# An encoder block on one core: both made-up weight sums are prepared in earlier stages and read back, and four more pairs of the down projection go by seven products

## The chip, the core and the metric

The kernel runs on one NeuronCore of a Trainium2 chip. The metric is the device time of one execution in microseconds (us). Five engines work side by side, each on its own list of instructions in order, and wait for each other by semaphores: TensorE (PE, with its weight loads as PEld), VectorE (DVE), ScalarE (ACT), GpSimd (POOL) and SyncE (SP). In this kernel SP and POOL issue the DMA transfers that matter here.

## The reference

One layer of an encoder on 256 tokens of width 2048, all in float32:

```python
h = rms_norm(x, attn_norm[i])
proj = h @ w_in[i]                                   # 10240 columns
ya = windowed_gqa(qa, ka, va, table, sink)
yb = dilated_attention(qb, kb, vb, table)
merged = sigmoid(ga) * (ya @ w_branch_a) + sigmoid(gb) * (yb @ w_branch_b)
x = x + merged @ w_out
hf = rms_norm(x, ffn_norm)
g = dwconv_centred(hf @ w_ffn_gate, conv_w, conv_b)  # 5632 columns
x = x + (gelu(g) * (hf @ w_ffn_up)) @ w_ffn_down     # down: 5632 -> 2048
gate_p = sigmoid(rms_norm(x, ple_norm) @ w_ple_gate)
x = x + gate_p * (p @ w_ple_proj)
return rms_norm(x, final_norm)
```

## The kernel before

Every float32 product is made of two halves of each operand: a rounded high half (`hi`) and the rest (`lo`). So each weight that is streamed from memory is split once: ACT copies it to `hi` (tiles `uh`, `vh`, line 305), DVE subtracts to get `lo` (tiles `ul`, `vl`, line 306), and PE multiplies with both. `thirds` is one product of a 128 x 128 block of the left side with 128 x 512 of the weights: three matmuls, lines 408 to 410 (`sh` by `wh`, `sh` by `wl`, `sl` by `wh`).

The weights come in 258 pieces of 128 x 2048 (1 MB), in the order in which they are used. SP loads a piece into one of three buffers `raw`; a piece's buffer is free for the piece three later when the last split of it is done. A piece is cut into units, and a unit's halves lie in a ring: six places for plain units (`u`), two for units that are made of sums (`v`). `pump` writes the splits into the program as soon as the ring has a place, and a scheduler then sets the final order on each engine, so a split can stand a long way ahead of its product.

The stages follow each other: A (projection and attention), B0 to B3 with ba and bb (gates and branches), D0 and D1 (output projection), E0 (first half of gate and up), F00 and F01 (first half of the down projection, to the left and the right 1024 columns), E1, F10 and F11 (second half), pp0 and pp1, G0, G2, G3 (the last gate). A down stage F works through 11 pieces, each a pair of k blocks by two blocks of 512 columns. A piece of kind `s` takes eight products (24 matmuls). A piece of kind `Z` takes seven (21 matmuls) by the method of Strassen and Winograd: M1 to M7, into seven PSUM banks, from four quarters of the weights and three sums of them, and from sums of the activations (`S`, made by `sums_of`). `DOWN` says which pieces are which.

For a Z piece one sum of three quarters is made ahead, in an earlier stage that has room: `sum_ahead` loads half of three quarters (POOL, line 268), two DVE additions make the sum (lines 271 and 272), POOL stores it in memory (line 275). One such half is an "ask" here. SP later reads the sum back into the first quarter of `raw` (line 255), beside the 768 KB of the other quarters (line 254). `sums_of_weights` makes the other three: line 282 makes the second quarter's (512 columns, after the quarter itself has been split as the piece's first unit), line 283 the third's and fourth's (1024 columns). The units of a Z piece are then: quarter 1 (512 columns), quarters 2 and 3 as they are (1024), `T21` (the first two sums) and `T03` (the last two). Asks run in stage A (16 of them, for D0 and D1), E0 (24, for F00 and F01) and E1 (28, for F10, F11 and G0), at most one for each job, a job being one block of 128 columns, 16 k blocks long. The buffers of the asks alternate between two places.

Of the kernel before, what the change touches and what calls it, by code (L numbers as in the profile page):

```python
# [16 lines left out]
P = 128  # L17
T = 256
# [77 lines left out]
DOWN = ("ZZsZsZsZsZs", "ZsZsZsZsZss")  # L96
# [97 lines left out]
def _encoder(ctx: ExitStack, tc, xt, pt, xrow, cols, gainrow, table, onehot, mask, ident_in, wts, out):  # L194
# [67 lines left out]
    def sum_ahead(p, h, tag):  # L262

        cols = slice(h * T, (h + 1) * T)
        if h == 0:
            ahead[p] = dram.tile([P, WIDE], F32, name="ahead%d" % p)
# [3 lines left out]
        def add():  # L270
            keep(nc.vector.tensor_tensor(q[:, 0], q[:, 2], q[:, 0], op=ALU.subtract))  # L271
            keep(nc.vector.tensor_tensor(q[:, 0], q[:, 0], q[:, 1], op=ALU.add))

        def store():
            keep(nc.gpsimd.dma_start(ahead[p][:, cols], q[:, 0]))
# [3 lines left out]
    def sums_of_weights(raw):  # L279

        q = [raw[:, i * WIDE:(i + 1) * WIDE] for i in range(4)]
        nc.vector.tensor_tensor(q[1], q[0], q[1], op=ALU.subtract)  # L282
        nc.vector.tensor_tensor(raw[:, 2 * WIDE:], raw[:, 2 * WIDE:], view(q[0], 0, (0, 2), (1, WIDE)), op=ALU.subtract)

    def produce():
# [13 lines left out]
        if kind == "T21" and not behind:  # L299
# [6 lines left out]
        nc.vector.tensor_tensor(lo, src, hi.bitcast(F32), op=ALU.subtract)  # L306
        if behind and u == _UNITS_OF[p][1]:
# [107 lines left out]
    def quad_stage(stage, moving, combos=None, tags=("M2", "M3", "M4", "P22")):  # L415
# [24 lines left out]
        for i, p in enumerate(pieces):  # L440
# [12 lines left out]
            else:  # L453
                s = combos(i)
                sums = [(s[:, 0, e], s[:, 1, e]) for e in range(4)]
# [37 lines left out]
    def gather(acc, scale=1.0, u=None, keep=lambda ins: ins):  # L493
# [3 lines left out]
        if u is None:  # L497
            u = sc.tile([P, T], F32, name="u")
# [32 lines left out]
    def diagonal(r):  # L531

        dg = sc.tile([P, T], F32, name="rdg", bufs=1)
# [316 lines left out]
    todo = [(p, h) for s in range(2) for p in _STAGES["D%d" % s] if _PIECES[p][0] == "Z" for h in range(2)]  # L850
# [67 lines left out]
    def sums_of(u, tag, s=None):  # L918
# [8 lines left out]
        if s is None:  # L927
            s = tok.tile([P, 2, 4, P], FR, name="S", tag="S%d" % tag)
        nc.scalar.activation(s[:, 0], f, AF.Copy)
        nc.vector.tensor_tensor(s[:, 1], f, s[:, 0].bitcast(F32), op=ALU.subtract)  # L930
# [120 lines left out]
    def places(half):  # L1051
# [6 lines left out]
        for i in seven[2:]:  # L1058
            d = act[:, at_:at_ + 14 * P].rearrange("p (c b t) -> p c b t", c=2, t=P)
            found[i] = lambda d=d: (d[:, :, :3], d[:, :, 3:])  # L1060
            at_ += 14 * P
        for i in eight[:-4]:
# [4 lines left out]
        for j, i in enumerate(seven[:2]):  # L1067
            found[i] = lambda j=j: (tok.tile([P, 2, 3, P], FR, name="ends", tag="S%d" % (2 + j)),
                                    tok.tile([P, 2, 4, P], FR, name="S", tag="S%d" % j))
        for j, i in enumerate(eight[-4:]):  # L1070
# [60 lines left out]
    ph_, pl_ = [], []  # L1131

# [4 lines left out]
    def split_last():  # L1137
        for k in range(2):
            ph_.append(sc.tile([P, T], FR, name="t"))
            pl_.append(sc.tile([P, T], FR, name="u"))  # L1140
            nc.scalar.activation(ph_[k], held["pr"][:, k], AF.Copy)
            nc.vector.tensor_tensor(pl_[k], held["pr"][:, k], ph_[k].bitcast(F32), op=ALU.subtract)
# [5 lines left out]
    for half in range(2):  # L1148
# [19 lines left out]
        if half:  # L1168
            at(("F10", 2, 0), load_last)
            at(("F10", 9, 0), split_last)  # L1170
# [26 lines left out]
    class Rows:  # L1197
# [3 lines left out]
        def __getitem__(self, i):  # L1201
            c = i[1]
            h = (ph_, pl_)[c.start >= T][self.k]
# [112 lines left out]
```

## Time and profile before

| | |
|---|---|
| runs | 1454.99 us median of 3 (1454.16 to 1456.2) |
| the profiled execution | 1455.38 us, its span 1453.6 us |
| granted TensorE clock | 0.998 |
| PE busy | 1442.5 us, 7470 matmuls |
| DVE busy | 1225.8 us |
| ACT busy | 827.7 us |
| POOL busy | 95.0 us |
| bytes moved | 318.57 MB, 219 GB/s on average |

The span is the time from the first to the last instruction; what the execution has beyond it (1.8 us) lies around the program. A row of the groups reads: line, engine, operation, tile written <- tiles read, shape, count | busy us, mean ns of one | idle time of the engine just before, and what ended it. Matmuls overlap in the records (each is shown with some 390 ns and the next begins before that), so the rate of PE is read from starts, not from durations. Waits of a matmul can also stand at its weight load (PEld).

### The profile page before, as it was taken

How to read it: one execution, taken by the hardware profiler on the slowest of the kernel's cores; microseconds unless marked ns; L12 is line 12 of the kernel's file. 1: busy time of each engine (PE TensorE's matmuls, PEld its weight loads, DVE VectorE, ACT ScalarE, POOL GpSimd, SP SyncE). 2: the span in 40 equal slices, each digit the busy share in tenths (PEclk: the TensorE clock that was granted, in tenths of full speed). 3: DMA queues.
4: the chain of work that ended last, by engine and by line, in shares of the span. 5: the costliest groups of instructions: out<-in, count | busy, mean ns of one | idle time of the engine just before them, and what ended most of it. 6: DMA issues, size and time to landing. Idle time of an engine off the chain costs nothing.

```text
span 1453.6 us, 19872 instructions
## 1 busy us (share of the span) xinstructions
PE 1442.5 (99%) x7470; PEld 1234.2 (85%) x7470; DVE 1225.8 (84%) x1754; ACT 827.7 (57%) x1148; POOL 95.0 (7%) x145
## 2 busy tenths in 40 slices
PE   9999999999999999999999999999999999999997
PEld 8888888888888888888888888888888888888885
DVE  7678775679998989889877999997878799998994
ACT  7455544546555655656545566465645466555753
POOL 0001120000000000000221100000221200000000
PEclk9999999999999999999999999999999999999999
DMA  9765575435556456465777655466776765556461
GB/s 331 273 211 201 199 262 188 172 142 203 188 190 233 179 217 238 174 253 209 270 238 273 237 210 194 189 249 226 265 281 236 261 241 213 199 196 233 173 249 69
DMA packets 62236, 318.57 MB, mean 219 GB/s; under 512 B 7668, under 2 KB 12660, under 8 KB 34236
## 3 DMA queue, kind: packets, MB, share of 16 engines
q1 hardware_dynamic: 50540, 280.46, 53.5%
q0 software_dynamic: 10880, 35.66, 6.8%
q8 instruction: 58, 0.95, 0.3%
q10 hardware_dynamic: 720, 1.19, 0.2%
q14 instruction: 38, 0.31, 0.1%
HBM read 306.23 MB, written 11.05 MB: 218 GB/s over the span
## 4 chain that ended last, share of the span: by engine, by line
PE 98%; DMA 0%; issue 0%; SPq 0%; ACT 0%; DVE 0%; POOLq 0%; POOL 0%; DVEq 0%
PE bank L351 29%; PE bank L358 15%; PE bank L408 14%; PE bank L409 14%; PE bank L410 14%; PE bank L397 2%; PE bank L399 2%; PE bank L398 2%; PE bank L335 2%; PE bank L336 1%; PE bank L947 1%; PE bank L756 0%; DMA raw<-in_wts 0%; PE bank L704 0%; PE bank L703 0%; PE bank L702 0%
## 5 line engine op out<-in xcount | busy, mean ns | idle before, releaser
L305 ACT ACTIVATE uh<-raw 128x1024 fp32r<-128x1024 f32 (+2 forms) x519 | 517.9, 1010 | 307.3 <-PE bank L410 112.5
L306 DVE TENSOR_TENSOR ul<-raw,uh 128x1024 fp32r<-128x1024 f32 (+2 forms) x519 | 594.6, 1164 | 95.7 <-ACT uh L305 66.8
L351 PE MATMUL bank<-hf,uh 128*128 128x512 f32 x1408 | 336.6, 391 | 0.0
L351 PEld LDWEIGHTS bank<-hf,uh 128*128 128x128 f32 x1408 | 258.8, 188 | 50.5 <-ACT uh L305 0.3
L358 PEld LDWEIGHTS bank<-hf,ul 128*128 128x128 f32 x1408 | 180.4, 191 | 6.7
L358 PE MATMUL bank<-hf,ul 128*128 128x256 f32 x1408 | 182.8, 283 | 0.0
L305 ACT ACTIVATE vh<-raw 128x1024 fp32r<-128x1024 f32 x96 | 100.9, 1056 | 55.5 <-DVE raw L282 27.8
L306 DVE TENSOR_TENSOR vl<-raw,vh 128x1024 fp32r<-128x1024 f32 x96 | 116.3, 1219 | 0.9
L351 PE MATMUL bank<-hs,uh 128*128 128x512 f32 x432 | 103.6, 392 | 0.0
L351 PEld LDWEIGHTS bank<-hs,uh 128*128 128x128 f32 x432 | 79.5, 188 | 15.6
L410 PE MATMUL bank<-uh,act 128*128 128x512 f32 x218 | 84.9, 390 | 0.0
L409 PE MATMUL bank<-ul,act 128*128 128x512 f32 x218 | 84.8, 389 | 0.0
L408 PE MATMUL bank<-uh,act 128*128 128x512 f32 x218 | 84.6, 390 | 0.0
L496 ACT ACTIVATE t<-bank 128x256 f32<-128x256 f32 x122 | 45.4, 374 | 59.1 <-PE bank L358 50.0
L408 PE MATMUL bank<-uh,hs 128*128 128x512 f32 x172 | 67.3, 392 | 0.0
L410 PE MATMUL bank<-uh,hs 128*128 128x512 f32 x172 | 67.2, 390 | 0.0
L409 PE MATMUL bank<-ul,hs 128*128 128x512 f32 x172 | 67.0, 389 | 0.0
L1092 ACT ACTIVATE gw<-gw,cl 128x256 f32<-128x256 f32 x44 | 24.1, 594 | 70.9 <-DVE gw L1089 70.8
L268 POOL DMA_DIRECT2D ahead<-in_wts x52 | 38.8, 747 | 379.0 <-DMA ahead<-ahead 210.0
L271 DVE TENSOR_TENSOR ahead<-ahead 128x256 f32<-128x256 f32 x52 | 22.0, 422 | 47.5 <-DMA ahead<-in_wts 47.4
L358 PE MATMUL bank<-hs,ul 128*128 128x256 f32 x432 | 56.6, 284 | 0.0
L358 PEld LDWEIGHTS bank<-hs,ul 128*128 128x128 f32 x432 | 54.5, 191 | 1.0
(270 smaller groups left out, 2454.1 us busy)
## 6 DMA issues: line engine op xcount, KB each, us to landing
raw<-in_wts SPq DMA_DIRECT2D x217, 1024.0 KB, 5.0
raw<-in_wts SPq DMA_DIRECT2D x34, 768.0 KB, 5.3
ahead<-in_wts POOLq DMA_DIRECT2D x52, 384.0 KB, 5.5
raw<-ahead SPq DMA_DIRECT2D x34, 256.0 KB, 5.3
ahead<-ahead POOLq DMA_DIRECT2D x52, 128.0 KB, 4.4
raw<-in_wts SPq DMA_DIRECT2D x12, 512.0 KB, 6.8
hb<-in_wts POOLq DMA_DIRECT2D x16, 384.0 KB, 5.4
ahead<-hb POOLq DMA_DIRECT2D x16, 128.0 KB, 4.6
```

The lines of the kernel that those rows point to most:

```text
L268: keep(nc.gpsimd.dma_start(q, wts[p][:, :3 * WIDE].rearrange("p (q c) -> p q c", c=WIDE)[:, :, cols]))
L305: nc.scalar.activation(hi, src, AF.Copy)
L306: nc.vector.tensor_tensor(lo, src, hi.bitcast(F32), op=ALU.subtract)
L335: nc.tensor.matmul(acc, hi[:, w], m, start=first, stop=False, skip_group_check=True)
L351: nc.tensor.matmul(acc, weights(u)[0][:, o * P:(o + 1) * P], m, start=first, stop=False, skip_group_check=True)
L358: nc.tensor.matmul(acc[:, T:], weights(u)[1][:, o * P:(o + 1) * P], m[:, :T], start=False, stop=last, skip_group_check=True)
L397: nc.tensor.matmul(acc[:, :n * P], xh, hi, start=(k == 0), stop=False)
L398: nc.tensor.matmul(acc[:, :n * P], xh, lo, start=False, stop=False)
L408: nc.tensor.matmul(acc, sh, wh, start=first, stop=False)
L409: nc.tensor.matmul(acc, sh, wl, start=False, stop=False)
L410: nc.tensor.matmul(acc, sl, wh, start=False, stop=last)
L496: keep(nc.scalar.activation(t, acc[:, T:], AF.Copy, scale=scale))
```

## The change

Both sums that can be made ahead are now made ahead. `sum_ahead` already formed the difference of two quarters on the way to the sum of three; it now keeps it (in the third quarter's place) and stores both. The first is read back by SP as before. The second is read back by POOL into the second quarter's place of `raw` (line 307 of the changed kernel), after that quarter has been split. Line 282 of before (512 columns on DVE for each Z piece) is gone.

With that the units of a Z piece are split in the order quarter 1, quarters 2 and 3, `T03`, `T21`, and the seven products take the order M1, M5, M4, M7, M6, M2, M3: the ones on `T03` come first, those on `T21`, which wait for the read back, later.

`DOWN` gets one more Z in each down stage: seven of eleven in F00 and F01, six of eleven in F10 and F11. That makes 38 Z pieces in all where 34 stood. The asks become 76 where 68 stood: 26 in A (D0, D1 and five of F00's seven pieces), 18 in E0, 32 in E1, where they now go round three places ("act2", "S4", "ends").

Smaller parts make room in SBUF: the additions' tile `u` moves to the attention pool, the diagonal tile shares the place of `t`, and `p` (the per-layer embedding) is split in one piece into a place of its own, in F11 and not in F10.

```diff
-DOWN = ("ZZsZsZsZsZs", "ZsZsZsZsZss")
+DOWN = ("ZZsZZsZZsZs", "ZZsZsZsZsZs")
...
         elif kind == "Z":
-            cuts = [("n", WIDE, 2 * WIDE), ("n", 2 * WIDE, 4 * WIDE), ("T21", 0, 2 * WIDE), ("T03", 2 * WIDE, 4 * WIDE)]
+            cuts = [("n", WIDE, 2 * WIDE), ("n", 2 * WIDE, 4 * WIDE), ("T03", 2 * WIDE, 4 * WIDE), ("T21", 0, 2 * WIDE)]
...
-            nc.sync.dma_start(raws[r][:, :WIDE], ahead.pop(r))
+            nc.sync.dma_start(raws[r][:, :WIDE], ahead[r][:, 0])
...
-            ahead[p] = dram.tile([P, WIDE], F32, name="ahead%d" % p)
+            ahead[p] = dram.tile([P, 2, WIDE], F32, name="ahead%d" % p)
...
-            keep(nc.vector.tensor_tensor(q[:, 0], q[:, 2], q[:, 0], op=ALU.subtract))
-            keep(nc.vector.tensor_tensor(q[:, 0], q[:, 0], q[:, 1], op=ALU.add))
+            keep(nc.vector.tensor_tensor(q[:, 2], q[:, 2], q[:, 0], op=ALU.subtract))
+            keep(nc.vector.tensor_tensor(q[:, 0], q[:, 2], q[:, 1], op=ALU.add))
...
-            keep(nc.gpsimd.dma_start(ahead[p][:, cols], q[:, 0]))
+            keep(nc.gpsimd.dma_start(ahead[p][:, :, cols], q[:, ::2]))
...
-        q = [raw[:, i * WIDE:(i + 1) * WIDE] for i in range(4)]
-        nc.vector.tensor_tensor(q[1], q[0], q[1], op=ALU.subtract)
-        nc.vector.tensor_tensor(raw[:, 2 * WIDE:], raw[:, 2 * WIDE:], view(q[0], 0, (0, 2), (1, WIDE)), op=ALU.subtract)
+        rest = raw[:, 2 * WIDE:]
+        nc.vector.tensor_tensor(rest, rest, view(raw[:, :WIDE], 0, (0, 2), (1, WIDE)), op=ALU.subtract)
...
-        if kind == "T21" and not behind:
+        if kind == "T03" and not behind:
             sums_of_weights(raw)
...
+        if _PIECES[p][0] == "Z" and u == _UNITS_OF[p][0]:
+            keep(nc.gpsimd.dma_start(raw[:, WIDE:2 * WIDE], ahead.pop(p)[:, 1]))
...
-                    todo = (("M1", m1, 0, 0, 0), ("M7", sums[2], 2, 1, None), ("M6", sums[1], 2, 0, 2),
-                            ("M5", sums[0], 3, 0, None), ("M4", m4, 3, 1, 3),
+                    todo = (("M1", m1, 0, 0, 0), ("M5", sums[0], 2, 0, None), ("M4", m4, 2, 1, 2),
+                            ("M7", sums[2], 3, 1, None), ("M6", sums[1], 3, 0, 3),
                             ("M2", m2, 1, 1, None), ("M3", sums[3], 1, 0, 1))
...
-    todo = [(p, h) for s in range(2) for p in _STAGES["D%d" % s] if _PIECES[p][0] == "Z" for h in range(2)]
+    todo = [p for s in ("D0", "D1", "F00") for p in _STAGES[s] if _PIECES[p][0] == "Z"]
+    todo = [(p, h) for p in todo for h in range(2)][:NA - START - 4]
...
-        todo = [(p, h) for p in sevens(half) for h in range(2)]
+        todo = [(p, h) for p in sevens(half) if p not in ahead for h in range(2)]
+        where = ("act2", "S4", "ends")[:2 + half]
         for i, (kind, n) in enumerate(jobs[joint:]):
-            if i > 1 and todo and (i % 2 == 0 or i < LASTS):
-                held["job"] = todo.pop(0), ("act2", "S4")[i % 2]
+            tag = where[i % len(where)]
+            if i > 1 and todo and (tag != "S4" or i < LASTS):
+                held["job"] = todo.pop(0), tag
```

The order in which the scheduler puts the instructions shows at three places. On PE, the first Z piece of F00 that follows an `s` piece (the fourth piece), before. Its first nine rows of 21 are M1, M7 and M6; `vh_8234` and `vl_8235` are T21:

```order
L408 MATMUL bank_8166<-uh_8207,act_5700 128x512
L409 MATMUL bank_8166<-ul_8208,act_5700 128x512
L410 MATMUL bank_8166<-uh_8207,act_5700 128x512
L408 MATMUL bank_8170<-vh_8234,act_5700 128x512
L409 MATMUL bank_8170<-vl_8235,act_5700 128x512
L410 MATMUL bank_8170<-vh_8234,act_5700 128x512
L408 MATMUL bank_8174<-vh_8234,act_5700 128x512
L409 MATMUL bank_8174<-vl_8235,act_5700 128x512
L410 MATMUL bank_8174<-vh_8234,act_5700 128x512
```

The same piece in the changed kernel, its first twelve rows: M1, then M5 and M4 on T03 (`vh_8256`), then M7 on T21 (`vh_8266`):

```order
L409 MATMUL bank_8188<-uh_8229,ends_6786 128x512
L410 MATMUL bank_8188<-ul_8230,ends_6786 128x512
L411 MATMUL bank_8188<-uh_8229,ends_6786 128x512
L409 MATMUL bank_8192<-vh_8256,S_6787 128x512
L410 MATMUL bank_8192<-vl_8257,S_6787 128x512
L411 MATMUL bank_8192<-vh_8256,S_6787 128x512
L409 MATMUL bank_8196<-vh_8256,ends_6786 128x512
L410 MATMUL bank_8196<-vl_8257,ends_6786 128x512
L411 MATMUL bank_8196<-vh_8256,ends_6786 128x512
L409 MATMUL bank_8204<-vh_8266,S_6788 128x512
L410 MATMUL bank_8204<-vl_8267,S_6788 128x512
L411 MATMUL bank_8204<-vh_8266,S_6788 128x512
```

So T21 is first read three products into the piece and no longer one.

On DVE, the making of that same piece (`raw_8100`) before: its two plain units, the two lines of sums, T21 and T03, with the next `s` piece (`raw_8194`) between:

```order
L306 TENSOR_TENSOR ul_8208<-raw_8100,uh_8207 128x512
L306 TENSOR_TENSOR ul_8220<-raw_8100,uh_8219 128x1024
L282 TENSOR_TENSOR raw_8100<-raw_8100 128x512
L283 TENSOR_TENSOR raw_8100<-raw_8100 128x1024
L306 TENSOR_TENSOR vl_8235<-raw_8100,vh_8234 128x1024
L306 TENSOR_TENSOR ul_8251<-raw_8194,uh_8250 128x1024
L306 TENSOR_TENSOR vl_8245<-raw_8100,vh_8244 128x1024
```

And after, where the next piece (`raw_8216`) is a Z piece too:

```order
L305 TENSOR_TENSOR ul_8230<-raw_8122,uh_8229 128x512
L305 TENSOR_TENSOR ul_8243<-raw_8122,uh_8242 128x1024
L305 TENSOR_TENSOR ul_8274<-raw_8216,uh_8273 128x512
L282 TENSOR_TENSOR raw_8122<-raw_8122 128x1024
L305 TENSOR_TENSOR ul_8285<-raw_8216,uh_8284 128x1024
L305 TENSOR_TENSOR vl_8257<-raw_8122,vh_8256 128x1024
L305 TENSOR_TENSOR vl_8267<-raw_8122,vh_8266 128x1024
```

One line of sums is left, both plain units of the next piece have moved ahead of this piece's sums' splits, and the read back of T21 has five rows between `ul_8230`, which frees the place, and `vl_8267`.

On POOL, the end of E0 before, where the stores of the last asks are followed by the loads of E1's:

```order
L275 DMA ahead172_7317<-ahead_7318 128x256
L275 DMA ahead172_7317<-ahead_7380 128x256
L268 DMA ahead_9154<-in_wts 128x3x256
L268 DMA ahead_9203<-in_wts 128x3x256
L275 DMA ahead218_9153<-ahead_9154 128x256
```

And after, with both planes in a store (256 rows) and the read backs of F00 behind it:

```order
L275 DMA ahead172_7035<-ahead_7036 256x1x256
L275 DMA ahead172_7035<-ahead_7088 256x1x256
L307 DMA raw_7947<-ahead152_2288 128x512
L307 DMA raw_7995<-ahead153_2425 128x512
L307 DMA raw_8122<-ahead155_2628 128x512
```

POOL, which issued nothing in D0, D1 and the F stages before, now issues one transfer for each Z piece there.

More of the change, by code (lines that the diff above doesn't have):

```diff
@@ L454, in quad_stage @@
                 s = combos(i)
-                sums = [(s[:, 0, e], s[:, 1, e]) for e in range(4)]
+                sums = [(t[:, 0, e], t[:, 1, e]) for t in s for e in range(t.shape[2])]
                 m1, m2, m4 = (part(a, 0), part(b, 0), part(b, 1)) if (stage, i) not in ends else ends[stage, i]
@@ L1068, in places @@
             found[i] = lambda j=j: (tok.tile([P, 2, 3, P], FR, name="ends", tag="S%d" % (2 + j)),
-                                    tok.tile([P, 2, 4, P], FR, name="S", tag="S%d" % j))
-        for j, i in enumerate(eight[-4:]):
+                                    [tok.tile([P, 2, 4, P], FR, name="S", tag="S%d" % j)])
+        for j, i in zip((0, 2, 3) if extra else range(4), eight[extra - 4:]):
             if j < 2:
@@ L1137, in split_last @@
     def split_last():
[L1138 to L1142, printed above, removed]
+        h = held["tok"].tile([P, 2, 2, T], FR, name="p", tag="S3")
+        held["p"] = h
+        nc.scalar.activation(h[:, 0], held["pr"], AF.Copy)
+        nc.vector.tensor_tensor(h[:, 1], held["pr"], h[:, 0].bitcast(F32), op=ALU.subtract)
     def sevens(half):
@@ L1168, in _encoder @@
         if half:
-            at(("F10", 2, 0), load_last)
-            at(("F10", 9, 0), split_last)
+            at(("F11", 2, 0), load_last)
+            at(("F11", 5, 0), split_last)
             held["ssq"] = sc.tile([P, 2, 2], F32, name="ssq", bufs=1)
```

29 lines of the change are left out of this document (18 added, 11 removed).

## The prediction

> **What bounds the kernel now.** I read the page's busy times first, then the chain that ended last, then PE's timeline for its real rate, then the four down stages one by one.
>
> ```profile
> PE 1442.5 (99%) x7470; PEld 1234.2 (85%) x7470; DVE 1225.8 (84%) x1754; ACT 827.7 (57%) x1148; POOL 95.0 (7%) x145
> PE 98%; DMA 0%; issue 0%; SPq 0%; ACT 0%; DVE 0%; POOLq 0%; POOL 0%; DVEq 0%
> ```
>
> PE carries 98% of the chain, so time is gained only by taking matmuls away or by closing gaps between them. What a matmul is worth is read from starts. The last piece of F00 is an `s` piece of 24 matmuls, and the next stage begins right behind it:
>
> ```profile
> 924.78 0.39 PE L408 MATMUL bank<-uh,act 128*128 128x512 f32 x1
> ...
> 930.22 0.39 PE L408 MATMUL bank<-uh,ends 128*128 128x512 f32 x1
> 930.45 0.39 PE L409 MATMUL bank<-ul,ends 128*128 128x512 f32 x1
> 930.67 0.39 PE L410 MATMUL bank<-uh,ends 128*128 128x512 f32 x1
> 931.18 0.47 PE L408 MATMUL bank<-vh,S 128*128 128x512 f32 x1
> ```
>
> 24 matmuls took 930.22 - 924.78 = 5.44 us, so one is worth 0.2267 us and not the 0.39 of its record; a product is 0.68, an `s` piece 5.44, a Z piece 21 x 0.2267 = 4.76. The last two rows show a gap: 0.51 where 0.23 is due.
>
> The down stages F00, F01, F10 and F11, cut where their first matmul starts:
>
> ```profile
> 874.18:930.22 56.04, 56.04 (x249) 46.11 (x247) 52.14 (x58) 32.34 (x37) 0.00 (x0) 1.00 0.54 196
> 930.22:986.52 56.30, 56.18 (x248) 46.02 (x246) 53.36 (x58) 30.70 (x34) 0.00 (x0) 1.00 0.61 225
> 1231.62:1288.09 56.47, 56.47 (x251) 46.75 (x250) 51.92 (x58) 32.25 (x38) 0.00 (x0) 1.00 0.57 208
> 1288.09:1346.00 57.91, 57.91 (x263) 47.82 (x261) 54.06 (x68) 34.60 (x44) 0.00 (x0) 1.00 0.59 218
> ```
>
> The columns are length, then busy time of PE, PEld, DVE, ACT and POOL, the granted clock (1.00), the DMA share and GB/s. F00 with six Z and five `s` should take 6 x 4.76 + 5 x 5.44 = 55.76 and takes 56.04; F01 56.30; F10 with five Z 56.44 and takes 56.47. So PE stands still for 0.28, 0.54 and 0.03 us there: almost nothing is left to close. DVE is the second engine, idle for only 3.90, 2.94, 4.55 and 3.85 us in a stage.
>
> **Four pieces by seven products.** Four pieces lose one product each: 4 x 3 x 0.2267 = 2.72 us off PE, at the clock of 1.00. This is the whole certain gain.
>
> **DVE and ACT in the down stages.** Durations of the splits and sums:
>
> ```profile
> L306 DVE TENSOR_TENSOR vl<-raw,vh 128x1024 fp32r<-128x1024 f32 x96 | 116.3, 1219 | 0.9
> L305 ACT ACTIVATE vh<-raw 128x1024 fp32r<-128x1024 f32 x96 | 100.9, 1056 | 55.5 <-DVE raw L282 27.8
> L283 DVE TENSOR_TENSOR raw<-raw 128x1024 f32<-128x1024 f32 x34 | 41.4, 1219 | 0.2
> L282 DVE TENSOR_TENSOR raw<-raw 128x512 f32<-128x512 f32 x34 | 23.4, 688 | 0.4
> L306 DVE TENSOR_TENSOR ul<-raw,uh 128x512 fp32r<-128x512 f32 x6 | 4.1, 688 | 3.5 <-ACT uh L305 3.4
> ```
>
> Before, a Z piece cost DVE 0.69 + 3 x 1.22 (splits) + 0.69 + 1.22 (sums) = 6.26, against 4.76 on PE; an `s` piece 2.44 against 5.44. Without line 282 a Z piece is 5.57. F00 and F01 go from 6 x 6.26 + 5 x 2.44 = 49.8 to 7 x 5.57 + 4 x 2.44 = 48.8; F10 and F11 from 45.9 to 45.6. PE's part falls by 0.68 in each. So DVE's room is kept within 0.4 us a stage, and in D0, D1 and G0 it grows by 4 x 0.69 = 2.8. ACT has 1.06 more for each of the added units and 40% of its time free.
>
> **The new pairs.** A pair ZZ stood at the start of F00 and F01 only; after the change eight pairs stand, three in each of F00 and F01, one in each of F10 and F11: six more. In a pair the second piece's sums can be split only when the first piece's places in the ring of two fall free. T03 falls free three products into the first piece and is needed one product into the second: 5 x 0.68 = 3.40 us for ACT 1.06 and DVE 1.22, so 1.1 us of room if both engines come at once. The price of a pair has two bounds: the 0.25 us by which F00 stands over F10, which starts without one, and nothing, since an in-stage pair finds DVE ahead of PE. I take 0.1 for each, as in-stage pairs are four of the six: 0.6 us (0 to 1.5).
>
> **The read back.** 38 transfers of 256 KB on POOL's queue, which was empty in these stages. The nearest rows:
>
> ```profile
> ahead<-in_wts POOLq DMA_DIRECT2D x52, 384.0 KB, 5.5
> raw<-ahead SPq DMA_DIRECT2D x34, 256.0 KB, 5.3
> ahead<-ahead POOLq DMA_DIRECT2D x52, 128.0 KB, 4.4
> L268 POOL DMA_DIRECT2D ahead<-in_wts x52 | 38.8, 747 | 379.0 <-DMA ahead<-ahead 210.0
> ```
>
> 256 KB lie between 4.4 and 5.5 us from issue to landing; I take 5.0. It is issued when the first unit is split; until T21's copy on ACT, a piece without a Z behind it has 1.22 (unit 2) + 1.22 (sums) + 1.06 (T03 on ACT) = 3.5 us of work, so ACT, and DVE behind it, would stand 1.5 us. In the pairs the order puts two units of the second piece between as well (0.69 + 1.22), and the transfer is covered. What hides the 1.5 us is the lead: in F10, T21 of the third Z piece was split at
>
> ```profile
> 1247.21 1.22 DVE L306 TENSOR_TENSOR vl<-raw,vh 128x1024 fp32r<-128x1024 f32 x1
> ```
>
> and its product came at 1231.62 + 2 x 4.76 + 2 x 5.44 + 0.68 = 1252.7, 4.3 us later; the new product order moves it 1.36 later still. I cost the read back at nothing (bounds 0 and 1.5 us a piece that has lost its lead). [...]
>
> **The reload chain.** The third-next piece's `raw` is loaded only when this piece's last unit is split (T03 before, T21 now), as DVE and SP show:
>
> ```profile
> 880.78 1.22 DVE L306 TENSOR_TENSOR vl<-raw,vh 128x1024 fp32r<-128x1024 f32 x1
> 882.03 0.33 SPq L257 DMA_DIRECT2D raw<-in_wts  x1
> raw<-in_wts SPq DMA_DIRECT2D x34, 768.0 KB, 5.3
> ...
> L305 ACT ACTIVATE uh<-raw x12: 612/1044/1065, 929.7 to 956.6; 128x1024 fp32r<-128x1024 f32 x9, 128x512 fp32r<-128x512 f32 x3
> ```
>
> From one pair's second piece to the next pair's second piece the chain is now: load 5.3, first unit 0.61 (ACT, the least of the last row, its 512 columns) + 0.69, read back 5.0, T21 1.06 + 1.22 = 13.9 us, against 2 x 4.76 + 5.44 = 14.96 of PE. It fits by 1.1 us. Its price is in the 0.6 above.
>
> **Asks.** A gets ten more, E0 six fewer, E1 four more, 0.42 + 0.42 of DVE each. E1 is the stage to look at:
>
> ```profile
> 986.52:1231.62 245.10, 245.10 (x1409) 216.39 (x1408) 203.89 (x331) 136.41 (x200) 37.02 (x56) 1.00 0.70 245
> L271 DVE TENSOR_TENSOR ahead<-ahead 128x256 f32<-128x256 f32 x28 | 11.8, 421 | 25.9 <-DMA ahead<-in_wts 25.9
> PEld bank L351 <- ACT uh L305: 0.3, 1, 0.3
> 1126.63 0.75 POOL L268 DMA_DIRECT2D ahead<-in_wts  x1 [4.38 <-DMA ahead<-ahead]
> 1127.77 0.57 POOL L275 DMA_DIRECT2D ahead<-ahead  x1 [0.39 <-DVE gw L500]
> 1132.59 0.74 POOL L268 DMA_DIRECT2D ahead<-in_wts  x1 [4.24 <-DMA ahead<-ahead]
> ```
>
> With two places, POOL waits some 4.3 us for a store before it may load the next ask, and DVE waits for that load: 25.9 us in 28 asks. That ran the weights' lead down until PE's loads waited for ACT once, 0.3 us. With three places the next load need not wait for the last store, so most of the 25.9 us go and the 4 x 0.84 = 3.4 us of the new asks fit. Gain on PE: 0.3 at most; I take 0.2. In A, DVE is busy for 34.02 of 54 us in the last stretch, so 10 x 0.84 is hidden:
>
> ```profile
> 250.00:304.00 54.00, 54.00 (x324) 48.16 (x323) 34.02 (x47) 28.13 (x39) 0.00 (x0) 1.00 0.50 182
> ```
>
> **F01's start.** The gap of 0.28 us before 931.18 is M7's bank, read by DVE at
>
> ```profile
> 930.35 0.68 DVE L900 TENSOR_TENSOR c<-bank,c 128x512 f32<-128x512 f32 x1
> ```
>
> Two lines 282 stand ahead of it on DVE and go (1.2 us), so this gap closes: 0.3 gained. The embedding's split, moved into F11, is one operation of 1024 elements for four of 256: nothing either way.
>
> **The sum.** -2.72 - 0.3 - 0.2 + 0.6 = -2.6 us. The profiled execution would go from 1455.38 to 1452.8; it stood 0.39 over the median, and from the median of 1454.99 I get 1452.4.
>
> **Rivals.** First, more comes back: pairs cost nothing and DVE's room in D0 and D1 closes what PE loses there to late splits. -2.72 - 0.5 - 0.3 = -3.5: 1451.5. For it speaks the shorter DVE work; against it, that PE has few gaps left.
>
> Second, the pairs take it back. If each of the six new ones costs the 0.25 of a stage's start, and the chain's 1.1 us of room is missed by half a microsecond at each of four turns, -2.72 - 0.5 + 1.5 + 2.0 = +0.3: 1455.3, no change. For it: F01's DVE has 2.94 us idle in all.
>
> Third, slower: the read back is what the in-order ACT and DVE wait for. If it takes the longest of the table (5.5) with 0.75 of issue, a lone Z piece stands 2.75 us. F10 and F11 have four lone ones each, F00 and F01 one: 10 x 2.75 = 27.5 us, less the stages' idle DVE time of 15.2 = 12.3 on PE, -2.7 + 12.3 = +9.6: 1464.6. It decides once the stages lose 5.6 us on PE, so from (15.2 + 5.6) / 10 = 2.1 us a piece, if no lead is left. Against it stand leads of 4 us and more, as above. [...]
>
> **How the numbers follow.** Forecast 0.60, 1451.6 to 1453.4; more back 0.16; pairs take it back 0.16; slower 0.08. 0.2% is 2.9 us, about what a measurement can tell from no change: 1452.1 is the edge, inside my forecast's own band, so of its 0.60 I count 0.26 as faster and 0.34 as within. Faster 0.42, within 0.50, slower 0.08. The range, 1450.9 to 1455.3, holds all but the slower case and a few per cent on each side.
>
> **What would show it.** Right: 12 matmuls of 128x512 fewer; F00 and F01 near 55.1 to 55.6, F10 and F11 near 55.9 and 57.5; no line 282 of 512 columns; DVE's wait for asks in E1 near nothing; F01's first gap gone. Wrong: ACT's `vh` waiting for `raw<-ahead`, followed by PE loads waiting for `vh`; gaps at the second pieces of pairs; an F stage longer than before.

## The result, and the profile after

The changed kernel takes 1490.09 us, median of 4 runs (1488.26 to 1499.71), where the kernel before took 1455.01 beside it: 1.0254 times as long, 95% interval 1.0209 to 1.0299. It is 35 us slower, not 2.6 faster. The profiled execution is the longest of the four (1499.7, span 1497.9), so the differences by stage below add up to some 43 us and not to 35.

The page after, its busy times and the chain that ended last by engine:

```profile
PE 1456.4 (97%) x7458; PEld 1235.4 (82%) x7458; DVE 1225.8 (82%) x1759; ACT 833.9 (56%) x1159; POOL 136.1 (9%) x199
PE 60%; DMA 13%; DVE 13%; issue 9%; ACT 3%; POOL 1%; SPq 0%; POOLq 0%; ACTq 0%; DVEq 0%
```

PE has the 12 matmuls fewer. But where it carried 98% of the chain it now carries 60%: transfers and DVE set the end in between. The stages D1, F00, F01, E1, F10 and F11 of the changed kernel (columns as in the prediction):

```profile
584.24:635.64 51.40, 46.95 (x197) 36.65 (x196) 40.96 (x47) 28.53 (x37) 1.62 (x3) 0.93 0.56 199
883.08:944.14 61.06, 57.71 (x245) 46.51 (x244) 51.34 (x53) 33.37 (x39) 3.77 (x7) 0.97 0.60 214
944.14:1004.17 60.03, 56.45 (x244) 45.14 (x243) 51.94 (x53) 32.70 (x36) 3.44 (x6) 1.00 0.66 235
1004.17:1256.96 252.79, 247.49 (x1408) 217.47 (x1409) 205.82 (x339) 135.38 (x201) 46.02 (x64) 0.99 0.75 261
1256.96:1319.41 62.45, 58.12 (x249) 45.65 (x247) 46.95 (x53) 30.53 (x37) 3.77 (x7) 1.00 0.59 211
1319.41:1386.13 66.72, 61.20 (x264) 48.61 (x262) 61.68 (x76) 40.58 (x52) 2.15 (x4) 0.95 0.57 209
```

D1 of the kernel before:

```profile
583.53:627.03 43.50, 43.50 (x197) 34.83 (x196) 39.69 (x49) 26.97 (x36) 0.00 (x0) 1.00 0.52 200
```

Against before D1 is 7.9 us longer, the four F stages 5.0, 3.7, 6.0 and 8.8, E1 7.7. G0 adds 3.2, A 0.6. E1's part belongs to this execution more than to the kernel: three other kernels with the read back (e1_ring, e2_four and e2_u5 below) have 245.01, 244.90 and 244.91 there. In F10 DVE is busy for 46.95 of 62.45 us: it has less work than before and stands still for 15.5 us where it stood for 4.55. So no engine has become the bound; they wait for each other. PE's weight loads wait for the splits of the sums (in us: total, times, the longest; before, the same two rows have 0.6 each):

```profile
PEld bank L410 <- DVE vl L305: 13.9, 15, 1.2
PEld bank L409 <- ACT vh L304: 10.3, 12, 2.4
```

What ACT waited for ahead of its splits in F00 and F01, before:

```profile
ACT uh L305 <- PE bank L410: 16.2, 8, 3.5
ACT uh L305 <- DMA raw<-in_wts: 0.6, 2, 0.4
```

and after:

```profile
ACT uh L304 <- DMA raw<-in_wts: 28.1, 12, 6.3
ACT uh L304 <- PE bank L411: 11.0, 5, 3.7
ACT vh L304 <- DMA raw<-ahead: 8.6, 4, 3.1
```

Before, ACT was ahead and waited for PE to free a place. After, it waits for data. The first of these three rows is not the read back's doing: e1_dve (below), the same kernel without it, has as much of it in the same two stages.

```profile
ACT uh L305 <- DMA raw<-in_wts: 30.6, 13, 6.4
```

What the read back adds is the last row, `vh` waiting for `raw<-ahead`: 26.7 us in 13 waits from D0 to G0. The lead, the time from the end of a split to the start of its product, was small already by the rest of the change. At the piece for which the prediction read a lead of 4.3 us (the third Z piece of F10), T21's split ends at 1252.62 us in e1_dve and its product starts at 1252.80; in the changed kernel it is 1278.40 and 1278.45.

The chain at the end of F10 and the start of F11 shows how the read back delays the splits:

```profile
1302.78 0.70 DVE ul L305
1303.47 0.40 issue
1303.88 4.93 DMA raw<-ahead
...
1308.97 1.07 ACT vh L304
...
1310.07 0.98 DVE vl L305
1311.05 0.16 issue
1311.21 1.83 DVE ul L305 x2
1313.04 0.30 issue
1313.34 6.97 DMA raw<-ahead
...
1320.47 1.06 ACT vh L304
...
1321.56 0.98 DVE vl L305
1322.54 0.16 issue
1322.70 1.22 DVE ul L305
1323.92 0.60 DVE c L904
1324.52 1.13 DVE raw L282
1325.65 0.61 DVE c L905
1326.26 0.04 issue
1326.31 0.80 PE bank L409
1327.10 0.43 PE bank L410
```

The landings stand in series. T21 waits for one; the first unit of the next Z piece stands behind T21 on DVE, and only that unit starts the next read back. From one read back to the next it is 9.46 us here, with a landing of 4.93. The read backs issued in F10, at 1257.82, 1269.73, 1281.57, 1292.62 and 1303.88, are 11.0 to 11.9 us apart, against 10.2 of PE for a Z and an `s` piece. (In a pair the order lets the second read back start before the first piece's T21; two run side by side there.) At the start of a stage the lines that free PE's banks (`c`, L904 and L905) stand behind the same wait, so PE stops there for 2.9 us more.

The stop in D1 ends with such a line too (`c`, L903). ACT's split waited for a landing, and DVE's `vl`, `ul` and `c` came behind it one after the other:

```profile
584.67 1.06 ACT L304 ACTIVATE vh<-raw 128x1024 fp32r<-128x1024 f32 x1 [2.57 <-DMA raw<-ahead]
588.87 0.47 PE L409 MATMUL bank<-vh,S 128*128 128x512 f32 x1 [3.78 <-DVE c L903]
```

PE's clock fell behind this stop of 3.78 us. The window behind it:

```profile
590.50:596.40 5.90, 5.83 (x14) 4.57 (x15) 5.90 (x9) 2.14 (x3) 0.54 (x1) 0.50 0.69 270
```

The granted clock is 0.50, and 14 matmuls take 5.90 us where 3.2 would do: 2.7 us on top of the stop. There are four such stretches (near 591, 924, 1191 and 1327 us); before has none but at the program's end, where both kernels have one (0.50 from 1447.52 us on, and from 1490.67 on in the changed kernel).

### The profile page after: what moved, and what is told of

The parts are those of the page before. It is cut to its first block, busy times and chain, and to the rows that moved or that the text cites. A ratio compares the mean times of both kernels' runs of the same rounds, so it can differ in the third digit from the quotient of the medians.

```text
span 1497.9 us, 20065 instructions
## 1 busy us (share of the span) xinstructions
PE 1456.4 (97%) x7458; PEld 1235.4 (82%) x7458; DVE 1225.8 (82%) x1759; ACT 833.9 (56%) x1159; POOL 136.1 (9%) x199
## 4 chain that ended last, share of the span: by engine, by line
PE 60%; DMA 13%; DVE 13%; issue 9%; ACT 3%; POOL 1%; SPq 0%; POOLq 0%; ACTq 0%; DVEq 0%
PE bank L352 17%; PE bank L359 9%; PE bank L410 8%; PE bank L409 8%; PE bank L411 8%; DMA raw<-ahead 6%; DVE ul L305 4%; DMA ahead<-in_wts 4%; DMA raw<-in_wts 2%; DVE vl L305 2%; PE bank L398 2%; PE bank L400 2%; PE bank L399 2%; ACT vh L304 2%; PE bank L336 2%
## 5 line engine op out<-in xcount | busy, mean ns | idle before, releaser
L305 DVE TENSOR_TENSOR ul<-raw,uh 128x1024 fp32r<-128x1024 f32 (+2 forms) x519 | 592.0, 1160 | 97.1 <-ACT uh L304 70.9
L305 DVE TENSOR_TENSOR vl<-raw,vh 128x1024 fp32r<-128x1024 f32 x104 | 125.7, 1221 | 37.4 <-ACT vh L304 37.2
L304 ACT ACTIVATE vh<-raw 128x1024 fp32r<-128x1024 f32 x104 | 108.3, 1056 | 73.1 <-DMA raw<-ahead 26.7
L307 POOL DMA_DIRECT2D raw<-ahead x38 | 20.6, 542 | 677.2 <-DVE ul L305 472.0
L409 PE MATMUL bank<-uh,act 128*128 128x512 f32 x192 | 74.9, 391 | 0.0
L410 PE MATMUL bank<-ul,act 128*128 128x512 f32 x192 | 74.7, 390 | 0.0
L411 PE MATMUL bank<-uh,act 128*128 128x512 f32 x192 | 74.5, 390 | 0.0
```

What stands on the lines that cost most here:

```text
L304: nc.scalar.activation(hi, src, AF.Copy)
L409: nc.tensor.matmul(acc, sh, wh, start=first, stop=False)
L410: nc.tensor.matmul(acc, sh, wl, start=False, stop=False)
L411: nc.tensor.matmul(acc, sl, wh, start=False, stop=last)
```

## The experiments

Times are medians; the ratio is to the kernel before in the same comparison, with its 95% interval.

| run | time | ratio | interval |
|---|---|---|---|
| changed kernel | 1490.09 | 1.0254 | 1.0209 to 1.0299 |
| e1_dve | 1462.91 | 1.0059 | 1.0040 to 1.0078 |
| e1_neither | 1461.16 | 1.0037 | 1.0024 to 1.0050 |
| e1_down | 1489.59 | 1.0239 | 1.0213 to 1.0266 |
| e1_ring | 1492.02 | 1.0249 | 1.0234 to 1.0264 |
| e2_elsewhere | 1467.89 | 1.0083 | 1.0066 to 1.0099 |
| e2_four | 1516.17 | 1.0412 | 1.0397 to 1.0428 |
| e2_u5 | 1516.90 | 1.0423 | 1.0404 to 1.0441 |
| e2_mid | 1466.48 | 1.0077 | 1.0054 to 1.0099 |
| e3_late | 1482.07 | 1.0179 | 1.0162 to 1.0196 |
| e3_order | 1461.76 | 1.0035 | 1.0022 to 1.0048 |
| e3_tail | 1457.54 | 1.0009 | 1.0000 to 1.0018 |
| e3_tail_old | 1455.33 | 0.9996 | 0.9987 to 1.0005 |
| e4_asks16 | 1463.21 | 1.0047 | 1.0031 to 1.0063 |
| e4_asks26 | 1455.75 | 0.9998 | 0.9989 to 1.0007 |
| e4_late_u5 | 1485.61 | 1.0205 | 1.0181 to 1.0229 |
| e4_late_four | 1493.53 | 1.0259 | 1.0231 to 1.0288 |
| e5_ring | 1458.00 | 1.0020 | 1.0007 to 1.0032 |
| e5_none | 1453.38 | 0.9980 | 0.9971 to 0.9989 |

**Is it the read back?** The second sum on DVE again (e1_dve), or not made at all (e1_neither):

```diff
+        nc.vector.tensor_tensor(raw[:, WIDE:2 * WIDE], raw[:, :WIDE], raw[:, WIDE:2 * WIDE], op=ALU.subtract)
...
-        if _PIECES[p][0] == "Z" and u == _UNITS_OF[p][0]:
-            keep(nc.gpsimd.dma_start(raw[:, WIDE:2 * WIDE], ahead.pop(p)[:, 1]))
```

The + line is in e1_dve alone.

> The changed kernel with the second sum made by DVE again (the 512-column subtraction of before) in place of POOL's read back; everything else as changed: seven, seven, six, six Z pieces, the new orders, asks on three places that store both sums. Theory A (the wait for the read back is what costs the down stages, D1 and G0): PE's stalls in F00, F01, F10, F11, D1 and G0 go, F00 and F01 take 55.1 to 56.5 us each where the changed kernel takes 61.1 and 60.0, D1 about 43.5 and not 51.4; E1 keeps its 252.8; 1458 to 1463 us in all. Rival B (the six new pairs and DVE's room cost it): DVE has 7 x 6.26 + 4 x 2.44 + 2.3 of other work = 55.9 us for 55.1 of PE in F00 and F01, so these stay at 59 us or more and the whole stays above 1475.

> The changed kernel without the read back and without any making of the second sum: the second half of T21 is the plain quarter, so this part of the computation is left out. It has the least DVE work and no wait. Theory A: as with the sum on DVE or 1 to 2 us better, 1457 to 1461, E1 still at 252.8. Rival B: pairs still starve for their places in the ring of two, more than 5 us of PE stalls left in F00 and F01. If the three readings 1458, 1458 and 1490 (neither, DVE, read back) come out, DVE's 0.69 was worth nothing and the read back cost all.

Both come back to 1461 to 1463 us: in place of the sum on DVE the read back costs 27 us. Rival B falls. Two things were not expected: some 7 us over the kernel before stay, and E1 has no stalls (244.9).

**Does it cost without the new pairs?** `DOWN` as before in the changed kernel:

```diff
-DOWN = ("ZZsZZsZZsZs", "ZZsZsZsZsZs")
+DOWN = ("ZZsZsZsZsZs", "ZsZsZsZsZss")
```

> The changed kernel with the down stages' pieces as before (six, six, five, five Z, one pair in F00 and in F01, none in F10 and F11), the read back and the new orders kept. Theory A: the read back costs without any new pair too: D1 stays near 51, the F stages stay 3 us or more above their 55.8 and 56.4, 1475 to 1490 in all. Rival B: with the pairs gone the stalls of the F stages go (under 1 us each), and only E1's 7 us and D1's 8 us stay: 1470 or less.

1489.59: as slow with 34 Z pieces as with 38. The pairs are not the cause.

**Traffic or waiting?** The same 38 transfers, to memory that nobody reads, and T21's second half from the plain quarter:

```diff
-            keep(nc.gpsimd.dma_start(raw[:, WIDE:2 * WIDE], ahead.pop(p)[:, 1]))
+            aside = dram.tile([P, WIDE], F32, name="aside%d" % p)
+            keep(nc.gpsimd.dma_start(aside, ahead.pop(p)[:, 1]))
```

> The changed kernel with POOL's read back sent to memory instead of the second quarter's place: the same 38 transfers of 256 KB at the same points of POOL's list, and nobody waits for their data; the second half of T21 is the plain quarter, so that part of the computation is left out. Theory A (the time that ACT, DVE and the reload of the same buffer wait for the landing): as without the read back, 1459 to 1464 us; no stall of PE above 1.5 us in D1 and F01. Rival E (the traffic itself, 38 more transfers on the same queues that slow SP's loads of weights): 1475 us or more, with SP's 768 KB loads at 6 us or longer.

1467.89 is 6.7 us over e1_neither, more than theory A allowed, and 22 under the changed kernel. But this run does not weigh the traffic, for the transfers did not run where the read backs do. The place in POOL's list is the same; with no buffer to wait for, POOL reached them early. The first goes out at 307.1 us, where the changed kernel's first goes out at 532.1:

```profile
L308 POOL DMA_DIRECT2D aside<-ahead x38: 526/535/672, 307.1 to 1373.3; - x38
```

They left in bursts: 8 at 307 to 314 us, 14 at 789 to 802, 13 at 1207 to 1220, each ahead of its stages, and 3 at 1372. Nor are all of the 6.7 us the price of their presence. This profile is 2.0 us behind that of e1_neither already at 224 us, after a stop of PE that ends at 213.68 (2.2 us against 1.1) and before any of them was issued; at the start of D0, with the first eight behind it, it is 2.1 us behind (545.30 against 543.22).

What the traffic does is read from SP's loads of weights in F00 and F01, in the changed kernel (KB each, median us from issue to landing):

```profile
raw<-in_wts SPq DMA_DIRECT2D x12, 1024.0 KB, 6.0
raw<-in_wts SPq DMA_DIRECT2D x11, 768.0 KB, 4.4
```

and in e1_dve, where no read back runs beside them:

```profile
raw<-in_wts SPq DMA_DIRECT2D x12, 1024.0 KB, 6.1
raw<-in_wts SPq DMA_DIRECT2D x11, 768.0 KB, 4.5
```

In these two stages the read backs do not slow the weights. That speaks against rival E; what is left is the wait.

**The buffer's loop or the standing in line?** Four buffers, with five places of the plain ring (e2_four), and their control with the first edit alone (e2_u5):

```diff
-RINGS = {"u": 6, "v": 2}
+RINGS = {"u": 5, "v": 2}
...
-            raws[r] = wpool.tile([P, PIECE * P], F32, name="raw", bufs=3)
+            raws[r] = wpool.tile([P, PIECE * P], F32, name="raw", bufs=4)
...
-        while state["raw"] < min(p + 3, _NPIECES):
+        while state["raw"] < min(p + 4, _NPIECES):
```

> The changed kernel, read back and all, with four buffers for the weight pieces in place of three, paid for with five places in place of six for the plain units' halves (both 8 KB per partition). Theory F (the loop of a buffer: load 5.2, first unit 1.3, read back 5.5 with its issue, T21 2.3, some 14.3 us and more with the waits in line, against 15 to 15.6 us that PE takes for three pieces): a fourth buffer gives the loop 20 us, and the down stages lose nearly all of their stalls: 27 us less than with three buffers, 1460 to 1468 against its control with five places and three buffers. Rival G (what costs is that ACT and DVE stand in line behind each landing, whatever the buffers): less than 10 us are gained over that control.

> Control for the run with four buffers: the changed kernel with five places for the plain units' halves and three buffers. Both theories: the read back's 27 to 34 us stay, and one unit less of lead costs something more, 1490 to 1500 us.

1516.17 against 1516.90: with five places a fourth buffer wins nothing, and theory F falls in this form. ACT's wait for weights in F00 and F01 goes from 6.1 us to 0.2 with it, and the time stays. That five places cost 27 us, far more than either theory allowed, points to the lead in units as what held the time down.

Then T21 moved in the list of units behind both units of the next piece (e3_late), so that the next piece's read back no longer waits for this one's:

```diff
+            if cut[0] == "T21":
+                late = p, cut
+                of[p].append(None)
+                continue
...
+            if late and late[0] < p and c == 1:
+                of[late[0]][3] = len(units)
+                units.append((late[0], *late[1]))
...
-        while state["raw"] < min(p + 3, _NPIECES):
+        first = min(q for q, *_ in _UNITS[u:u + 4])
+        while state["raw"] < min(first + 3, _NPIECES):
```

> The changed kernel, read back and three buffers kept, with T21 of a Z piece moved in the list of units behind both units of the next piece, so that DVE has five or six operations (some 6 us) between the one that starts the read back and T21's, where it had three or four (3.5 us). The weights' next load starts later by that. Theory G (what costs is that ACT and DVE stand in line behind each landing): the landing of 5.0 to 5.5 us is covered, ACT's wait for it (26.7 us by the groups) falls under 8 us and the stalls of D1, F and G0 mostly go: 1461 to 1468 us. Rival F in its other form (the buffer's loop is too long): a loop made longer costs more, 1490 us or above.

1482.07: 8 us better, on neither theory's value. ACT's wait for the landing, from D0 to G0, was 26.7 us in 13 waits and is now

```profile
ACT vh L315 <- DMA raw<-ahead: 18.4, 9, 3.4
```

The direction is theory G's, and with this order five places cost 3.5 us and not 27:

> Control: the kernel with the read back and T21 behind both units of the next piece (1482.1 us) with five places in place of six for the plain units' halves. Both theories: slower than with six, 1495 to 1515 us.

> The control before this one with four buffers for the weight pieces. If the loop of a buffer is what is left once T21 is covered: 10 us or more faster than the control. If it is the standing in line: within 4 us of it.

1485.61, and with the fourth buffer 1493.53, 8 us more, which neither theory expected. So the loop is not what is left either. Where e3_late's 19 us over e1_dve lie was not settled.

**E1 and the room for descriptors.** In E1 POOL waited for its own loads. 1152 bytes for descriptors:

```diff
-    nc = bacc.Bacc("TRN2", target_bir_lowering=False, num_devices=1, dynamic_dma_scratch_size=1024)
+    nc = bacc.Bacc("TRN2", target_bir_lowering=False, num_devices=1, dynamic_dma_scratch_size=1152)
```

> The changed kernel with 1152 bytes in place of 1024 for the descriptors of POOL's transfers, nothing else. In E1 each ask's load was issued 0.34 us after the load before it had landed, though its place was free several us earlier. Theory C: the descriptors of a load (384 rows), a store (256 rows) and one more load do not fit together; 128 bytes more let them, the loads are issued without that wait, DVE's wait for asks falls from about 50 us to under 15, E1's stalls (7.4 us) go and E1 takes 245 to 246.5; 1480 to 1484 in all. Rival D: the loads wait for something else, or the transfers themselves are slow (up to 8.6 us), and E1 stays at 250 or more, 1487 to 1492 in all. The F stages do not change by either.

POOL's waits for its asks, in the changed kernel (E1):

```profile
POOL ahead L268 <- DMA ahead<-in_wts: 88.0, 22, 6.6
```

in e1_ring, around E1 (990 to 1260 us), where no row of waits for loads is left:

```profile
POOL ahead L268 <- DMA ahead<-ahead: 31.3, 11, 5.5
```

and E1 of e1_ring:

```profile
1005.11:1250.12 245.01, 245.01 (x1408) 216.56 (x1409) 208.08 (x345) 138.72 (x202) 46.87 (x65) 1.00 0.79 272
```

Theory C is borne out in the waits: with 128 bytes more the 88.0 us in 22 waits are gone. The 6 to 10 us are not: the time is 1492.02, no better. E1 also took 244.9 in e1_dve, e2_four and e2_u5, which have 1024 bytes and 70.9, 73.4 and 77.0 us of the same waits of POOL: they held nothing up there. The traces agree on three sides: with two sums stored and 1024 bytes the waits are there (88.0 us in the changed kernel, 71.8 in e3_order), with 1152 bytes no row of them is left (e1_ring, e5_ring), and with one sum stored and 1024 bytes there is none either (the kernel before, e4_asks26). That the descriptors of a load, a store and one more load fill the room, as the theory has it, and how many bytes each takes, is not shown.

**The other 7 us.** The pair of F10 and F11 moved to the middle (e2_mid, from e1_dve):

```diff
-DOWN = ("ZZsZZsZZsZs", "ZZsZsZsZsZs")
+DOWN = ("ZZsZZsZZsZs", "ZsZsZsZZsZs")
```

> The kernel with the second sum on DVE (1462.9 us) with the new pair of F10 and F11 moved from their start into their middle (ZsZsZsZZsZs). Theory H: the stall of 2.6 us at F10's third product (M4's and M2's neighbours wait for a bank that DVE frees only behind the pair's sums) and about 1 us at F11's start go, and nothing takes their place: 1459 to 1460.5 us. Rival: DVE's work is the same, so the stall only moves to the pair's new place: 1462 to 1464.

1466.48, a miss: F10 still stops, now for 2.7 and 1.9 us, and the clock is 0.50 for 6.8 us behind the first stop. The order of the units, as before (e3_order, from e1_dve):

```diff
-... ("T03", 2 * WIDE, 4 * WIDE), ("T21", 0, 2 * WIDE)]
+... ("T21", 0, 2 * WIDE), ("T03", 2 * WIDE, 4 * WIDE)]
...
-                    todo = (("M1", m1, 0, 0, 0), ("M5", sums[0], 2, 0, None), ("M4", m4, 2, 1, 2),
-                            ("M7", sums[2], 3, 1, None), ("M6", sums[1], 3, 0, 3),
+                    todo = (("M1", m1, 0, 0, 0), ("M7", sums[2], 2, 1, None), ("M6", sums[1], 2, 0, 2),
+                            ("M5", sums[0], 3, 0, None), ("M4", m4, 3, 1, 3),
```

> The kernel with the second sum on DVE (1462.9 us) with the units and products of a Z piece in the order of before (T21 before T03; M7 and M6 before M5 and M4). If the reordering cost part of the 7 us over the kernel before: 1458 to 1460 us, with F10 and F11 nearer to 56. If the order does not matter where nothing is read back: 1461.5 to 1464.5 us, F10's stall of 2.6 us still there.

F10 in e1_dve:

```profile
1232.05:1290.90 58.85, 56.39 (x249) 45.97 (x248) 54.04 (x63) 33.77 (x40) 0.00 (x0) 1.00 0.54 197
```

and in e3_order, with the same pieces:

```profile
1232.08:1287.89 55.81, 55.81 (x249) 46.19 (x247) 52.22 (x59) 32.33 (x37) 0.00 (x0) 1.00 0.54 198
```

The stop is gone in this profile by the order alone; the medians, 1461.76 and 1462.91, do not tell the two apart. Then one sum stored for each ask, 16 asks in A, F00 and F01 as before and six Z in F10 and F11 (e3_tail), and that in the old order (e3_tail_old):

```diff
-DOWN = ("ZZsZZsZZsZs", "ZZsZsZsZsZs")
+DOWN = ("ZZsZsZsZsZs", "ZsZsZZsZZss")
...
-            keep(nc.gpsimd.dma_start(ahead[p][:, :, cols], q[:, ::2]))
+            keep(nc.gpsimd.dma_start(ahead[p][:, 0, cols], q[:, 0]))
...
-    todo = [p for s in ("D0", "D1", "F00") for p in _STAGES[s] if _PIECES[p][0] == "Z"]
+    todo = [p for s in ("D0", "D1") for p in _STAGES[s] if _PIECES[p][0] == "Z"]
```

> A version without the read back: the second sum on DVE, one sum stored for each ask, 16 asks in A as before, F00 and F01 as before (six Z), F10 and F11 with six Z placed ZsZsZZsZZss, so that the tenth pair stays of eight products as before; new order of products. 6 matmuls of 128x512 fewer than before (-1.36 us). Theory I (F10's stall came from the tenth pair: its sums of activations stand on DVE before the operation that frees the bank for M2): the stall at F10's start is under 0.5 us, and the time is 1453.5 to 1456 us. Rival (DVE is late there for the asks and the sums, whichever pair it is): F10 still stalls by 2 us or more, 1457 to 1460 us.

> The run before this one with the units and products of a Z piece in the order of the kernel before. If the reordering is free without a read back: within 1 us of it. If it costs: 1452.5 to 1455 us and the faster of the two; by theory I and the 6 matmuls fewer, 1453.7 us.

1457.54 and 1455.33: the new order costs 2.2 us, also where nothing is read back. F10 takes 55.8 us in both, without a stop. With e3_order that makes two ways out of F10's stop, the old order or a tenth pair of eight products with one sum stored; theory I was not settled. Last, 38 Z pieces (`DOWN` as changed) with one sum stored in the old order, by the asks in A. The line `todo` is that of e3_tail for 16 asks (e4_asks16) and that of the changed kernel for 26 (e4_asks26):

> No read back: the second sum on DVE, one sum stored for each ask, units and products of a Z piece in the order of before, the changed kernel's 38 Z pieces, and 16 asks in A, 28 in E0, 32 in E1. Theory J (in the runs before this one the ten asks more in A cost some 5 us and more from run to run, since DVE waits there for their loads ahead of work that PE needs): 1453 to 1455.5 us, runs within 2 us of each other; the 12 matmuls fewer give up to 2.7 us. Rival (the 38 Z pieces themselves starve DVE): 1458 us or more.

> The run before this one with the changed kernel's asks: 26 in A, 18 in E0, 32 in E1. Theory J: 4 to 7 us slower than with 16, 1458 to 1462 us, runs scattered over 4 us or more, a stall of 1 us or more of PE near 212 us. Rival: within 1.5 us of the run with 16.

1463.21 and 1455.75: theory J falls, the other way round. With 28 asks in E0, on two places, F00 stops for 5.2 us at its start, and the clock is 0.50 for 3.4 us behind that; with 26 in A there is neither. From e3_order to e4_asks26 the only edit is the store, 1461.76 to 1455.75: storing both sums costs 6 us, or 5.4 by the ratios. Where they lie on PE is not seen, since the execution in e3_order's profile took 1456.74. In E1 DVE waited for its asks (19.8 us in e3_order), in the changed kernel and in e4_asks26:

```profile
L271 DVE TENSOR_TENSOR ahead<-ahead 128x256 f32<-128x256 f32 x32 | 13.5, 421 | 32.0 <-DMA ahead<-in_wts 31.9
```

```profile
L271 DVE TENSOR_TENSOR ahead<-ahead 128x256 f32<-128x256 f32 x32 | 13.4, 420 | 0.7 <-DMA ahead<-in_wts 0.7
```

Then e3_order with 1152 bytes for descriptors (e5_ring):

> The kernel with both sums stored, the second made on DVE and the order of units as before (1461.8 us), with 1152 bytes in place of 1024 for POOL's descriptors. Theory K (the six us of storing both sums come from the loads that wait for room for their descriptors, 71.8 us in 21 waits in E1): 1455.5 to 1457 us. Rival (the larger stores themselves, on the queues that bring the weights): 1460 us or more, and the waits for loads gone from POOL all the same.

1458.00 (1.0007 to 1.0032) lies between both and on neither: how much of the 6 us is room for descriptors and how much is bytes stays open. DVE's wait for asks in E0 and E1 stays at 38.7 us with the room (38.0 without it, 18.7 with one sum stored), so the larger store has its part. And e4_asks26 without the second sum, which leaves that part of the computation out (e5_none):

```diff
-        nc.vector.tensor_tensor(raw[:, WIDE:2 * WIDE], raw[:, :WIDE], raw[:, WIDE:2 * WIDE], op=ALU.subtract)
```

> The kernel with 38 Z pieces, one sum stored, the order of before, 26 asks in A (1455.75 us) without the second sum, neither made nor read: the second half of T21 is the plain quarter, so this part of the computation is left out. It bounds what a free read back could bring. If DVE's 38 x 0.69 us took the gain of the 12 matmuls: 1452.5 to 1454 us, F00 and F01 near 55.2. If not: 1455 to 1456.5 us.

1453.38, 2.1 us under the kernel before, its F00:

```profile
875.09:930.29 55.20, 55.20 (x243) 45.69 (x244) 50.17 (x51) 33.51 (x38) 0.00 (x0) 1.00 0.58 202
```

Of the kernels that compute the whole, none was faster than the one before by more than the measurement tells. One edit at a time, the medians go from 1490.09 (changed kernel) to 1462.91 (second sum on DVE), 1461.76 (old order), 1455.75 (one sum stored) and 1453.38 (no second sum): 27, 1, 6 and 2 us.

## Why the prediction was wrong

- Step that failed first: "I cost the read back at nothing (bounds 0 and 1.5 us a piece that has lost its lead)". It costs 27 us (changed kernel against e1_dve). The 1.5 us of waiting were near the mark (ACT waited for 13 of the 38, 2.1 us each); the wrong part was that a lead of 4.3 us, read at one piece of the kernel before, would hide it. Other pieces of that kernel had no such lead: the prediction's own row of 880.78 ends at 882.00, and the product of that split starts at 882.39. And the rest of the change had used the lead up at the piece that was read: 0.2 us in e1_dve, without a read back. The splits that waited for a landing then held PE up, as the rows of PE's loads and the chain above show.
- "The reload chain ... fits by 1.1 us" asked the wrong chain. A fourth buffer changed nothing. The chain from one read back to the next through the line on DVE was not added up: 11.0 to 11.9 us in F10 against 10.2. That this chain alone decides is argued from the profile; e3_late, which breaks it, won 8 of the 27 us.
- The third rival had the mechanism and the sign (ACT and DVE stand in line; 1464.6) but was given 0.08, and was too low by 25 us: it counted lone pieces of the F stages and took DVE's idle time of before off as if it could be used. D1, G0, the bank-freeing lines behind the wait, and the half clock were not in it.
- "Gain on PE: 0.3 at most; I take 0.2" for the asks left out that each store became twice as large. Three places do end DVE's wait, as forecast, but with one sum stored (0.7 us); with both it is 32.0, and storing both makes the time 6 us longer (e3_order against e4_asks26).
- "The new pairs ... 0.6": not refuted. With one sum stored and the old order three pairs stand in F00, and it takes 56.12 against an ideal of 55.09; without DVE's second sum 55.20.
- "Four pieces by seven products, 2.72": right. 7458 matmuls; and e5_none, where everything that was given back is left out, is 2.1 us faster than before by the medians (1.6 to 4.2 by the interval). The forecast of -2.6 is what a read back that cost nothing, with nothing more to store, would have brought.
- F01's first gap: gone as forecast (its first piece takes 4.79 us against 4.76), and of no weight.
- The landing itself was costed right: POOL's 38 read backs took 5.0 us in the median (3.0 to 8.4), and 5.0 was taken.

## What to carry to other kernels

A transfer in the middle of a chain that in-order engines prepare ahead is to be costed per piece, in series with the next one, against the time of a piece. A lead read at one piece in the profile of before is no cover: read it at every piece, and ask what the rest of the change does to it. Add up the chain from one such transfer to the next through everything that stands in line between them, and look for what else is behind it: here the lines that free PE's banks. To a stop of PE add the half clock that can follow; in the changed kernel it came to four stretches of 3.41 to 6.83 us (next section). And before a run is read as a control, look in its profile whether the thing that was kept still happens at the same time.

## What was not expected of the hardware

The half clock: in the changed kernel 128x512 matmuls start 0.43 us apart behind the longer stops, where 0.23 is usual, until the clock returns. The clock is 0.50 from 589.55, 924.06, 1190.30 and 1323.42 us on, for 6.83, 3.41, 3.41 and 6.83 us. The starts are 98, 78 and 39 times 3.413 us apart: in this trace all changes of the clock lie on one grid of 3.413 us.

In the step of that grid ahead of each of the four PE stood still for 2.82, 2.14, 3.32 and 2.65 us (a 128x512 matmul counted as 0.2267 us from its start), and for 2.88 ahead of the fall at the program's end; in the steps at full clock that no fall follows, from 5.87 us on, where the record begins, for 1.72 at most. The stop of 2.10 us that ends at 962.37 left the clock as it was: the grid cuts it at 961.61, into 1.34 and 0.76. So a fall went here with what stood within one step, not with the length of a stop.

The same count over all profiles of this case has 2.05 us or more in each of the 41 steps ahead of a fall; of the steps at full clock that no fall follows, all but five have less than 1.9 us, and those five 2.04 to 2.31. From 2.05 to 2.31 us, then, it went either way. The 2.4 us of e3_late (1380.8), behind which the clock fell, lie within one step; the 2.6 us of e1_dve (1235.3), behind which it did not, are cut in two, 1.85 in the fuller one.

POOL's loads in E1 stood still until the load before had landed, though the store that frees their place had landed before: at 1157.02 for the load of 1161.00, which came 0.34 us behind the landing of the load before at 1160.66. With 128 bytes more for descriptors that ended: e1_ring has no row of POOL waiting for a load there.
